# A two-block transformer on one core: the bias row spread by DRAM, three norms' roots applied after the products, padded key pairs

## The chip, the core and the metric

One core of a Trainium2 chip runs the whole program: one launch, all weights read from HBM. TensorE (PE) multiplies; VectorE (DVE), ScalarE (ACT) and GpSimd (POOL) do the elementwise work; SyncE (SP) and POOL issue most DMAs. Each engine works through its own queue in the order in which the program issues the instructions; semaphores order the queues against each other. The metric is the device time in microseconds (us), lower is better.

## What is computed

256 tokens of width 1024 in float32 go through two blocks. Cut to what matters here:

```python
# block 1
h = rms_norm(x, norm_mix_g)
u, q, keys and values (4 groups, 16 heads of 64), gates = split(h @ w_in)
conv = depthwise causal conv (31 taps), layer_norm, silu, @ conv_pw_w
s = q k / 8 + rel_bias[t5_bucket(tq - tk)]      # selected and windowed attention: 16 heads x 256 x 256
y = sigmoid(g_conv) * conv + sigmoid(g_attn) * nsa
x = x + y @ w_out
x = x + cross_attention(rms_norm(x, norm_x_g), mem)        # xq_w, xkv_w, xo_w
a, b = split(rms_norm(x, norm_ffn_g) @ ffn_in_w);  x = x + (silu(a) * b) @ ffn_out_w
x = rms_norm(x, final_norm_g)
# block 2
u, v, q, k, v2 = split(rms_norm(x, norm1_g_2) @ w_in_2)
mix = [u * spatial_gating(v), dilated_attention(rope(q), rope(k), v2)]   # 8 heads of 64
x = x + mix @ w_out_2
x = x + peer(rms_norm(x, norm2_g_2))            # 16384 experts, top 16 of 8 heads
out = rms_norm(x, final_norm_g_2)
```

A norm is `x * g / sqrt(mean(x^2) + eps)`: one factor per token, the root, and one per channel, the gain.

## The kernel before

**Products.** Float32 is split into two float32r parts, `hi` (a rounded copy) and `lo` (the rest); a product is three passes, hi*hi, hi*lo, lo*hi. The activations of a stage lie transposed (`hh`, `hl`: channels on partitions, 256 tokens in the row). `form2` makes outputs with channels on partitions (24 passes of 256 columns for a unit of weights), `form1` outputs with tokens on partitions (12 passes of 512 columns). `cols2`, `cols1` and `rows_c` run them over all units of a weight.

**The stream.** `Stream` (line 37) loads weights in chunks of 1 MB into three raw buffers; half a chunk is a unit. For each unit ACT casts `hi` (line 96) and DVE subtracts to `lo` (line 107) into one of four pairs of buffers (six from the cross-attention to w_out_2). `st.next` asks for as many units ahead as there are pairs less one, the subtraction one unit less. `st.split` does all its casts, then all its subtractions. Evacuations are put off to the next `st.next` (`st.defer`).

**The tail of a stage.** `rows_c` keeps the last four units and runs them output by output (two token blocks `tt`, two halves `hf`), then calls `finish` (line 302): `evac` adds to the residual x, multiplies by the gain into `xg` and squares with a sum; `root` gives the factor (power -0.5 on POOL, line 407) and a diagonal matrix from it (line 409); `mid` is a product in between; `turn` transposes `xg` on PE in two groups of four blocks, by multiplying with the diagonal (`by`, line 363, a float32 product in two passes) or with `ident` (line 361), then copies `hi` on ACT (line 367) and subtracts `lo` on DVE (line 368). Between the two turns stands one `st.split`, behind them another. Five stages end so: conv_pw_w (no norm), w_out (norm_x, with the product `mem_keys(3)` as `mid`), xo_w (norm_ffn), ffn_out_w (two norms one after the other, lines 1008 to 1035) and w_out_2 (norm2).

**The bias.** A product of the bias table with one-hot buckets gives a row per head (line 471). It is stored to DRAM (`b_dram`, line 477) and read back so that partition p begins at element p (`brev`, line 482). That is upside down, so eight products with a flip matrix (line 505), one per unit of w_u from the second step on, put it right. Behind the reads, in POOL's queue, stand a memset of `vpad` and the loads of the convolution's constants (`dww`, line 487, `cvec`). The convolution runs in the background on ACT (first tap, line 512) and DVE (30 taps, line 515), a few taps behind each unit.

**The scores.** `qT` and `ksw` hold two heads' channels on 128 partitions. A score product takes 64 of them, at partition 0 or 64 (lines 724 and 1148), 32 jobs in block 1 (half of them with 512 columns, half with 256) and 16 in block 2.

## Time and profile before

| | us |
|---|---|
| median of 3 runs | 1568.57 (1566.01 to 1569.83) |
| profiled execution, its own time | 1568.51 |
| its span | 1566.74 |
| PE busy | 1535.3 (98%) |
| DVE busy | 1108.8 (71%) |
| ACT busy | 830.1 (53%) |
| DMA moved | 262.79 MB, mean 168 GB/s |

A row of the trace names a line of the kernel, an engine, an operation and the tiles `out<-in`. Passes on PE overlap: from the start of one to the start of the next is less than the time from its start to its end. "Chain" rows give the time that a piece holds up the end. An arrow `<-` in brackets says what ended the idle time before an instruction. Float32 operands (not split) take two passes of PE for one product.

### The profile page before, as it was taken

How to read it: one execution, taken by the hardware profiler on the slowest of the kernel's cores; microseconds unless marked ns; L12 is line 12 of the kernel's file. 1: busy time of each engine (PE TensorE's matmuls, PEld its weight loads, DVE VectorE, ACT ScalarE, POOL GpSimd, SP SyncE). 2: the span in 40 equal slices, each digit the busy share in tenths (PEclk: the TensorE clock that was granted, in tenths of full speed). 3: DMA queues.
4: the chain of work that ended last, by engine and by line, in shares of the span. 5: the costliest groups of instructions: out<-in, count | busy, mean ns of one | idle time of the engine just before them, and what ended most of it. 6: DMA issues, size and time to landing. Idle time of an engine off the chain costs nothing.

```text
span 1566.7 us, 25104 instructions
## 1 busy us (share of the span) xinstructions
PE 1535.3 (98%) x9990; PEld 1373.9 (88%) x9990; DVE 1108.8 (71%) x2058; ACT 830.1 (53%) x1330; POOL 37.2 (2%) x75
## 2 busy tenths in 40 slices
PE   7999999999999999999999999999999999999998
PEld 7998777779799987877999999999999888888886
DVE  5887888665555555765899868999995555555555
ACT  5443565745454444465444557776664444444443
POOL 2010000000000000100000000000000000000000
PEclk9999999999999999999999999999999999999999
DMA  8454212454355563642545543433335655555552
GB/s 316 168 190 162 80 63 83 151 201 175 108 188 189 187 216 113 259 148 93 182 171 185 184 162 138 153 141 135 137 138 211 233 198 200 188 188 193 200 198 82
DMA packets 38870, 262.79 MB, mean 168 GB/s; under 512 B 4688, under 2 KB 4848, under 8 KB 8672
## 3 DMA queue, kind: packets, MB, share of 16 engines
q1 hardware_dynamic: 34992, 248.72, 44.4%
q0 software_dynamic: 2752, 9.32, 1.7%
q10 hardware_dynamic: 1008, 3.15, 0.6%
q8 instruction: 78, 1.28, 0.3%
q14 instruction: 40, 0.33, 0.1%
HBM read 257.99 MB, written 2.13 MB: 166 GB/s over the span
## 4 chain that ended last, share of the span: by engine, by line
PE 92%; DVE 4%; ACT 2%; issue 1%; DMA 1%; POOL 0%; POOLq 0%; SPq 0%; ACTq 0%; DVEq 0%
PE mm L250 41%; PE mm L270 12%; PE mm L271 12%; PE mm L272 12%; PE tp L1385 4%; PE tp L250 3%; PE tp L724 2%; PE pv L759 1%; DVE lo L107 1%; PE tp L1148 1%; PE tp L746 1%; DMA raw<-in_w_qkv_dram 0%; PE tp L1287 0%; PE tp L505 0%; ACT hi L96 0%
## 5 line engine op out<-in xcount | busy, mean ns | idle before, releaser
L96 ACT CAST hi<-raw 128x1024 fp32r<-128x1024 f32 x427 | 445.8, 1048 | 446.8 <-PE mm L272 214.4
L107 DVE TENSOR_TENSOR lo<-raw,hi 128x1024 fp32r<-128x1024 f32 x427 | 516.9, 1219 | 93.1 <-ACT hi L96 91.4
L250 PE MATMUL mm<-xnt,hi 128*128 128x256 f32 x2416 | 434.6, 282 | 9.2 <-ACT hi L96 8.6
L250 PEld LDWEIGHTS mm<-xnt,hi 128*128 128x128 f32 x2416 | 370.1, 188 | 10.3 <-ACT hi L96 8.6
L250 PE MATMUL mm<-xnt,lo 128*128 128x256 f32 x1208 | 338.0, 280 | 0.5 <-DVE lo L107 0.5
L250 PEld LDWEIGHTS mm<-xnt,lo 128*128 128x128 f32 x1208 | 227.6, 188 | 0.8 <-DVE lo L107 0.8
L270 PE MATMUL mm<-hi,wring 128*128 128x512 f32 x512 | 199.3, 389 | 1.2 <-ACT wring L243 1.2
L271 PE MATMUL mm<-lo,wring 128*128 128x512 f32 x512 | 199.3, 389 | 0.1
L272 PE MATMUL mm<-hi,wring 128*128 128x512 f32 x512 | 199.3, 389 | 0.1
L250 PE MATMUL mm<-hh,hi 128*128 128x256 f32 (+1 forms) x992 | 180.2, 283 | 1.0 <-DVE hh L368 1.0
L250 PEld LDWEIGHTS mm<-hh,hi 128*128 128x128 f32 (+1 forms) x992 | 151.5, 186 | 5.7 <-issue 4.3
L250 PE MATMUL mm<-hh,lo 128*128 128x256 f32 (+1 forms) x496 | 138.5, 279 | 0.0
L244 DVE TENSOR_TENSOR wring<-act,wring 128x512 fp32r<-128x512 f32 x64 | 44.2, 693 | 123.9 <-ACT wring L243 123.9
L270 PEld LDWEIGHTS mm<-hi,wring 128*128 128x128 f32 x512 | 96.1, 188 | 21.2 <-ACT wring L243 1.4
L271 PEld LDWEIGHTS mm<-lo,wring 128*128 128x128 f32 x512 | 96.1, 188 | 20.6 <-DVE lo L107 0.6
L272 PEld LDWEIGHTS mm<-hi,wring 128*128 128x128 f32 x512 | 96.1, 188 | 20.3 <-DVE wring L244 0.5
L515 DVE SCALAR_TENSOR_TENSOR cacc<-vpad,dww,cacc 128x256 f32<-128x256 f32 x240 | 100.9, 479 | 6.3 <-ACT cacc L512 6.3
L250 PEld LDWEIGHTS mm<-hh,lo 128*128 128x128 f32 (+1 forms) x496 | 92.6, 187 | 0.0
L1391 DVE TENSOR_TENSOR act<-act,tp 128x208 f32<-128x208 f32 (+31 forms) x64 | 57.6, 922 | 12.9 <-PE tp L1385 10.5
L270 PE MATMUL mm<-hi,hh 128*128 128x512 f32 x156 | 64.6, 414 | 0.0
L96 ACT CAST hi_x<-raw 128x1024 fp32r<-128x1024 f32 x40 | 41.9, 1051 | 41.7 <-PE mm L250 17.8
L271 PE MATMUL mm<-lo,hh 128*128 128x512 f32 x156 | 61.9, 397 | 1.5 <-DVE lo L107 1.5
(384 smaller groups left out, 2174.5 us busy)
## 6 DMA issues: line engine op xcount, KB each, us to landing
raw<-in_expert_u_dram SPq DMA_DIRECT2D x64, 1024.0 KB, 4.8
raw<-in_expert_v_dram SPq DMA_DIRECT2D x64, 1024.0 KB, 4.8
raw<-in_ffn_in_w_dram SPq DMA_DIRECT2D x22, 1024.0 KB, 4.8
raw<-in_ffn_out_w_dram SPq DMA_DIRECT2D x11, 1024.0 KB, 4.8
raw<-in_w_u_dram SPq DMA_DIRECT2D x8, 1024.0 KB, 6.6
raw<-in_w_g_dram SPq DMA_DIRECT2D x8, 1024.0 KB, 4.8
raw<-in_w_out_dram SPq DMA_DIRECT2D x8, 1024.0 KB, 4.9
raw<-in_w_query_dram SPq DMA_DIRECT2D x8, 1024.0 KB, 4.9
```

Of the source, the lines that this page charges most:

```text
L96: self.nc.scalar.copy(out=hi, in_=raw)
L107: self.nc.vector.tensor_tensor(out=lo, in0=raw, in1=hi.bitcast(F32), op=ALU.subtract)
L244: V.tensor_tensor(out=lo, in0=src, in1=hi.bitcast(F32), op=ALU.subtract)
L250: T.matmul(out=ps, lhsT=a, rhs=b, start=(k == 0), stop=(k == n - 1))
L270: T.matmul(out=ps, lhsT=a, rhs=r, start=first and k == 0, stop=False)
L271: T.matmul(out=ps, lhsT=a, rhs=q, start=False, stop=False)
L272: T.matmul(out=ps, lhsT=b, rhs=r, start=False, stop=last and k == nk - 1)
L515: V.scalar_tensor_tensor(out=cacc[:, j, :], in0=vpad[:, j, w:w + S], scalar=dww[:, j, w:w + 1], in1=cacc[:, j, :], op0=ALU.mult, op1=ALU.add)
L724: T.matmul(out=sv, lhsT=qT[po:po + 64, (g // 2) * 4 + r, tt * P:(tt + 1) * P], rhs=ksw[po:po + 64, g // 2, :, 0:n], start=True, stop=True)
L746: T.transpose(out=tps[:, o:o + P], in_=pr[:, br, c * P:(c + 1) * P], identity=ident)
L1385: T.matmul(out=ps[:, j * P:(j + 1) * P], lhsT=ring[:, b % 2, 0, j, :], rhs=ring[:, b % 2, 1, j, :], start=True, stop=True)
L1391: V.tensor_tensor(out=o[:, :, 0:there], in0=o[:, :, 0:there], in1=pv[:, :, 0:there], op=ALU.mult)
```

## The change

Three edits.

**Bias.** The table is tiled eight times, so that the product gives the row on 128 partitions (384 columns in place of 512). Eight DMAs write each head's row 128 times to DRAM, two read it back with a step of 383, which lays the bias the right way round into `bias`. The flip matrix and its eight products are gone.

**Norms.** `tail` replaces `finish` in all five stages: the first tokens are turned before the last quarter of the products. norm_x, norm_ffn and the pair behind ffn_out_w turn `x * gain` with `ident`, without the root. For the first two `row` spreads the roots along a row with a product of ones and the diagonals, and the evacuations of xq_w and ffn_in_w multiply by it; for the third the roots are per-partition scales in block 2's evacuations. With `hold` the last quarter of the turning is put off into the next stage's first product (`run_late`): half-way through the first unit of `form2`, or at the third unit of `cols1`.

**Scores.** `ksw` and `dk` keep each key twice: head 0's channels with zeros below, head 1's with zeros above; a score product contracts all 128 partitions.

```diff
+    pending = []
+
+    def run_late():
+
+        while pending:
+            pending.pop(0)()
+
...
+    def tail(pp, prod, evac, turn, root=None, after=None, mid=None, hold=False):
+
+
+
+
+
+        for hf in range(2):
+            prod(0, hf, 0, 4)
+            evac(0, hf, pp[0][hf])
+        if root is not None:
+            root(0)
+        prod(1, 0, 0, 4)
+        evac(1, 0, pp[1][0])
+        turn(0, (0, 4))
+        prod(1, 1, 0, 3)
+        st.split(max(st.n_high, st.n_used + 1))
+        if root is None:
+            turn(1, (0,))
+        prod(1, 1, 3, 4)
+        evac(1, 1, pp[1][1])
+        if root is not None:
+            root(1)
+            turn(1, (0,))
         if mid is not None:
             mid()
-        if turn is not None:
-            turn(0)
-        st.split(max(st.n_high, st.n_used + 1))
-        if turn is not None:
-            turn(1)
+        if hold:
+            pending.append(lambda: turn(1, (4,)))
+        else:
+            turn(1, (4,))
         st.split(st.n_used + st.ahead)
         st.flush()
+        if after is not None:
+            after(0)
+            after(1)
 
...
+        def after(tt):
+            rs[tt] = wk.tile([P, 1], F32, tag="rs1", name="rs1")
+            V.tensor_scalar(out=rs[tt], in0=ss[tt][:, 0:1], scalar1=ss[tt][:, 1:2], scalar2=D * EPS, op0=ALU.add, op1=ALU.add)
+            nc.gpsimd.tensor_tensor(out=rs[tt], in0=rs[tt], in1=expo[:, 0:1], op=ALU.pow)
+
+        def row(scale):
+            ps = tp_tile()
+            for tt in range(2):
+                dg = wk.tile([P, P], F32, tag="diag", name="diag")
+                V.tensor_scalar(out=dg, in0=ident, scalar1=rs[tt], scalar2=32.0 * scale, op0=ALU.mult, op1=ALU.mult)
+                T.matmul(out=ps[:, tt * P:(tt + 1) * P], lhsT=ones_1, rhs=dg, start=True, stop=True)
+            out = rrow_p.tile([P, S], F32, tag="rrow", name="rrow")
+            A.copy(out=out, in_=ps[:, 0:S])
+            return out
+
...
     b_ps = tp_tile()
-    T.matmul(out=b_ps[0:16, :], lhsT=rb, rhs=oneh, start=True, stop=True)
-    V.tensor_tensor(out=brow, in0=b_ps[0:16, :], in1=brow, op=ALU.add)
+    T.matmul(out=b_ps[:, 0:LB], lhsT=rb, rhs=oneh, start=True, stop=True)
+    V.tensor_tensor(out=brow, in0=b_ps[:, 0:LB], in1=brow, op=ALU.add)
     turn(0)
     drive(key_steps[1])
     turn(1)
-    b_dram = tc.dram_tile([16, 512], F32, name="b_dram")
-    nc.gpsimd.dma_start(out=b_dram, in_=brow)
-    b_ap = b_dram[:, :]
-    brev = []
-    for n, (pool, tag) in enumerate(((m1, "qT"), (res, "xv"))):
-        t = pool.tile([P, 8, S], F32, tag=tag, name="brev")
-        nc.gpsimd.dma_start(out=t, in_=bass.AP(tensor=b_ap.tensor, offset=b_ap.offset + n * 8 * 512, ap=[[1, P], [512, 8], [1, S]]))
-        brev.append(t)
+    b_dram = tc.dram_tile([16, P, LB], F32, name="b_dram")
+    for r in range(8):
+        nc.gpsimd.dma_start(out=b_dram[:, 16 * r:16 * r + 16, :], in_=bc(brow[16 * r:16 * r + 16, :].unsqueeze(1), [16, 16, LB]))
+    b_ap = b_dram[:, :, :]
+    for n in range(2):
+        nc.gpsimd.dma_start(out=bias[:, 8 * n:8 * n + 8, :],
+                            in_=bass.AP(tensor=b_ap.tensor, offset=b_ap.offset + n * 8 * P * LB + P - 1,
+                                        ap=[[LB - 1, P], [P * LB, 8], [1, S]]))
     vpad = m1.tile([P, KK, CW - 1 + S], F32, tag="vpad", name="vpad")
     nc.gpsimd.memset(vpad[:, :, 0:CW - 1], 0.0)
...
-            T.matmul(out=sv, lhsT=qT[po:po + 64, (g // 2) * 4 + r, tt * P:(tt + 1) * P],
-                     rhs=ksw[po:po + 64, g // 2, :, 0:n], start=True, stop=True)
+            T.matmul(out=sv, lhsT=qT[:, (g // 2) * 4 + r, tt * P:(tt + 1) * P],
+                     rhs=ksw[:, g // 2, g % 2, :, 0:n], start=True, stop=True)
...
+    ends, row = scaled_norm(x, gain_tile("norm_x_g"), nh, nl, xg)
+    rows_c("w_out", 4, yh, yl, **ends, mid=lambda: all_of(mem_keys(3, 0)))
+    rrow = row(1.0 / 16)
...
-        A.activation(out=t.rearrange("p c t -> p (c t)"), in_=ps, func=ACTF.Copy, scale=1.0 / 16)
+        V.tensor_tensor(out=t, in0=ps.rearrange("p (c t) -> p c t", c=2), in1=bc(rrow.unsqueeze(1), [P, 2, S]), op=ALU.mult)
...
+            if not rrows:
+                rrows.append(row(1.0))
+            ab = f2.tile([P, 2, S], F32, tag="ab", name="ab")
+            V.tensor_tensor(out=ab, in0=ps.rearrange("p (c t) -> p c t", c=2), in1=bc(rrows[0].unsqueeze(1), [P, 2, S]), op=ALU.mult)
             hid = f2.tile([P, S], F32, tag="hid", name="hid")
-            A.activation(out=hid, in_=ps[:, 0:S], func=ACTF.Silu)
-            V.tensor_tensor(out=hid, in0=hid, in1=ps[:, S:2 * S], op=ALU.mult)
+            A.activation(out=hid, in_=ab[:, 0], func=ACTF.Silu)
+            V.tensor_tensor(out=hid, in0=hid, in1=ab[:, 1], op=ALU.mult)
...
+    def after4(tt):
+        ssq = wk.tile([P, 2], F32, tag="ss2", name="ssq")
         r = wk.tile([P, 1], F32, tag="rs2", name="rs2")
-        V.tensor_tensor(out=t, in0=ssq[tt][:, :, 0], in1=ssq[tt][:, :, 1], op=ALU.add)
-        V.scalar_tensor_tensor(out=r, in0=t[:, 0:1], scalar=EPS, in1=t[:, 1:2], op0=ALU.mult, op1=ALU.add)
+        junk = [f1.tile([P, D], BF16, tag="junk4", bufs=2, name="junk4") for _ in range(2)]
+        A.activation(out=junk[0], in_=x[:, tt, :], func=ACTF.Square, accum_out=ssq[:, 0:1])
+        V.tensor_tensor(out=x[:, tt, :], in0=x[:, tt, :], in1=gains[0], op=ALU.mult)
+        A.activation(out=junk[1], in_=x[:, tt, :], func=ACTF.Square, accum_out=ssq[:, 1:2])
+        V.scalar_tensor_tensor(out=r, in0=ssq[:, 0:1], scalar=EPS, in1=ssq[:, 1:2], op0=ALU.mult, op1=ALU.add)
         V.tensor_scalar(out=r, in0=r, scalar1=1.0 / D, scalar2=EPS * EPS, op0=ALU.mult, op1=ALU.add)
-        nc.gpsimd.tensor_tensor(out=r, in0=r, in1=expo[:, 0:1], op=ALU.pow)
-        dgs[tt] = wk.tile([P, P], F32, tag="diag", name="diag")
-        V.tensor_scalar(out=dgs[tt], in0=ident, scalar1=r, scalar2=None, op0=ALU.mult)
-        rstd_of(t[:, 0:1], t[:, 0:1], 1.0 / D, 1)
-        r1s[tt] = t[:, 0:1]
-
-    def turn4(tt):
-        transpose_split(xg[:, tt, :], hh, hl, tt, by=dgs[tt])
-        V.tensor_scalar(out=x[:, tt, :], in0=xg1[:, tt, :], scalar1=r1s[tt], scalar2=None, op0=ALU.mult)
-
-    rows_c("ffn_out_w", DFF // 256, fh, fl_, evac=evac4, root=root4, turn=turn4)
+        nc.gpsimd.tensor_tensor(out=r2[tt][:, 0:1], in0=r, in1=expo[:, 0:1], op=ALU.pow)
+        V.tensor_scalar(out=r2[tt][:, 1:2], in0=r2[tt][:, 0:1], scalar1=0.125, scalar2=None, op0=ALU.mult)
+        rstd_of(ssq[:, 0:1], ssq[:, 0:1], 1.0 / D, 1)
+        V.tensor_scalar(out=x[:, tt, :], in0=x[:, tt, :], scalar1=ssq[:, 0:1], scalar2=None, op0=ALU.mult)
+
+    rows_c("ffn_out_w", DFF // 256, fh, fl_, evac=evac4, after=after4, hold=True,
+           turn=lambda tt, groups: transpose_split(xg[:, tt, :], hh, hl, tt, groups=groups))
...
+            if c == 2:
+                run_late()
```

## Rows read from the trace of the kernel before

**Rows 1.** Page, part 1: busy us, share of the span, instructions of each engine.
```profile
PE 1535.3 (98%) x9990; PEld 1373.9 (88%) x9990; DVE 1108.8 (71%) x2058; ACT 830.1 (53%) x1330; POOL 37.2 (2%) x75
```

**Rows 2.** Waits of PE: who waited for whom, us in total, times, longest.
```profile
PE tp L363 <- DVE rs L339: 2.4, 1, 2.4
```

**Rows 3.** Windows: length; busy of PE, PEld, DVE, ACT, POOL (instructions); granted clock, DMA, GB/s.
```profile
135.00:235.00 100.00, 99.32 (x524) 73.84 (x522) 85.25 (x245) 58.97 (x152) 0.00 (x0) 1.00 0.27 97
...
437.00:560.00 123.00, 123.00 (x1036) 122.50 (x1035) 69.15 (x87) 61.63 (x88) 0.00 (x0) 1.00 0.55 190
```

**Rows 4.** Chain that ended last, in order of time: start us, us, what.
```profile
37.13 2.83 PE mm L250 x24
...
39.95 0.86 PE tp L505 x2
...
151.38 1.05 PE tp L724 x2
...
694.66 0.63 PE tp L1148 x2
```

**Rows 5.** Timeline of PE: start us, us, engine, line, operation, out<-in, count.
```profile
376.92 1.89 PE L250 MATMUL tp<-xk,xq 128*128 128x256 f32 x8
```

**Rows 6.** Timeline of PE, then DVE, behind w_out's products (norm_x).
```profile
360.20 3.73 PE L363 MATMUL tp<-diag,xg 128*128 128x128 f32 x32
...
365.63 0.38 PE L250 MATMUL tp<-xnl,hi_x 128*128 128x256 f32 x1 [0.99 <-DVE xnl L368]
...
364.89 1.28 DVE L368 TENSOR_TENSOR xnl<-tp,xnh 128x512 fp32r<-128x512 f32 x2
...
366.08 4.62 DVE L107 TENSOR_TENSOR lo<-raw,hi 128x1024 fp32r<-128x1024 f32 x4
```

**Rows 7.** Timeline of POOL: the transfers that it issues, 24 to 30 us.
```profile
24.07 0.55 POOL L477 DMA_DIRECT2D b_dram<-brow  x1 [3.47 <-DVE brow L472]
...
27.35 1.82 POOL L482 DMA_DIRECT2D brev<-b_dram  x2 [2.73 <-DMA b_dram<-brow]
...
29.40 0.57 POOL L487 DMA_DIRECT2D dww<-in_conv_dw_w_dram  x1
```

**Rows 8.** Tiles brev, then dww: us from issue to landing.
```profile
DMA to landing us min/median/max: 7.2/9.7/12.2
...
DMA to landing us min/median/max: 12.3/12.3/12.3
```

**Rows 9.** Timeline of ACT, then DVE, at the convolution's first steps.
```profile
45.01 1.09 ACT L512 ACTIVATE cacc<-vpad,cvec,dww 128x256 f32<-128x256 f32 x2
...
45.65 1.76 DVE L515 SCALAR_TENSOR_TENSOR cacc<-vpad,dww,cacc 128x256 f32<-128x256 f32 x4 [3.14 <-ACT cacc L512]
```

**Rows 10.** DMA queues in 34 to 38 us: packets, MB, share of 16 engines.
```profile
q1 hardware_dynamic: 125, 1.02, 65.2%
...
q0 software_dynamic: 147, 0.60, 38.0%
```

**Rows 11.** Groups by line: transposes by ident; count, busy us, mean ns.
```profile
L361 PE MATMUL tp<-ident,mixo 128*128 128x128 f32 x16 | 2.4, 275 | 0.0
```

**Rows 12.** Timeline of DVE, then PE, around w_out_2's last products.
```profile
729.13 0.29 DVE L409 TENSOR_SCALAR diag<-ident,rs 128x128 f32<-128x128 f32 x1 [0.66 <-POOL rs L407]
...
730.89 1.95 PE L363 MATMUL tp<-diag,xg 128*128 128x128 f32 x16
```

**Rows 13.** Timeline of PE behind ffn_out_w's products; in brackets idle time before.
```profile
617.26 1.95 PE L363 MATMUL tp<-diag,xg 128*128 128x128 f32 x16
...
621.60 2.05 PE L363 MATMUL tp<-diag,xg 128*128 128x128 f32 x16 [2.39 <-DVE rs L339]
...
623.40 0.48 PE L270 MATMUL mm<-hi,hh 128*128 128x512 f32 x1
```

**Rows 14.** Windows: the last 4.5 us; then the chain at the start.
```profile
1562.20:1566.70 4.50, 0.00 (x0) 0.00 (x0) 0.49 (x1) 0.72 (x1) 0.01 (x1) 0.51 0.31 117
...
9.85 9.73 PE mm L250 x70
```

More of the change, by code (lines that the diff above doesn't have):

```diff
@@ L33 @@
 CF = 2048
+LB = 384
 HF = CF // 2
@@ L255, in form2 @@
         wl = w[1].rearrange("p (k n) -> p k n", k=KK)
-        pairs = []
         for k in range(KK):
-            a, b = wh[:, k, :], wl[:, k, :]
-            pairs += [(a, hh[:, k, :]), (a, hl[:, k, :]), (b, hh[:, k, :])]
-        mm3(ps, pairs)
+            if k == KK // 2:
+                run_late()
+            for n, (a, b) in enumerate(((wh, hh), (wh, hl), (wl, hh))):
+                T.matmul(out=ps, lhsT=a[:, k, :], rhs=b[:, k, :], start=k == 0 and n == 0, stop=k == KK - 1 and n == 2)
     def form1(ps, w, hh, hl, ks, nk, tt, n0, n, first, last):
@@ L330, in rows_c, with prod @@
         ws = [st.next(name, st.ahead - c) for c in range(4)]
-        for tt in range(2):
-            for hf in range(2):
-                for c in range(4):
-                    form1(pp[tt][hf], ws[c], ah, al, n - 4 + c, 1, tt, hf * 512, 512, n == 4 and c == 0, c == 3)
-        finish(pp, **ends)
+        def prod(tt, hf, c0, c1):
+            for c in range(c0, c1):
+                form1(pp[tt][hf], ws[c], ah, al, n - 4 + c, 1, tt, hf * 512, 512, n == 4 and c == 0, c == 3)
+        tail(pp, prod, **ends)
     def rstd_of(dst, ss, scale, n):
@@ L501, in tile_model @@
     nc.gpsimd.memset(cbias, NEG)
-    def bias_flip(c):
-        ps = tp_tile()
-        T.matmul(out=ps, lhsT=flip, rhs=brev[c // 4][:, 2 * (c % 4):2 * (c % 4) + 2, :].rearrange("p h k -> p (h k)"), start=True, stop=True)
-        st.defer(lambda: A.copy(out=bias[:, 2 * c:2 * c + 2, :].rearrange("p h k -> p (h k)"), in_=ps))
     cacc = m1.tile([P, KK, S], F32, tag="cacc", name="cacc")
@@ L536, in glu_evac @@
         return evac
-    flips = iter(range(8))
     for j in range(KK):
@@ L541, in tile_model @@
             run_bg(B[0])
-            c = next(flips, None) if j else None
-            if c is not None:
-                bias_flip(c)
     nc.gpsimd.tensor_copy(out=cbias[:, 0, :, 0:7], in_=bias[:, :, 159::16])
@@ L969, in tile_model, with x_prod @@
     ws = [st.next("xo_w", st.ahead - k) for k in range(2)]
-    for tt in range(2):
-        for hf in range(2):
-            for k in range(2):
-                form1(xo[tt][hf], ws[k], oh_, ol_, 6 + k, 1, tt, hf * 512, 512, False, k == 1)
+    def x_prod(tt, hf, c0, c1):
+        for k in range(c0 // 2, c1 // 2):
+            form1(xo[tt][hf], ws[k], oh_, ol_, 6 + k, 1, tt, hf * 512, 512, False, k == 1)
     hh, hl = parts_of(ht_p, "hh", False)
-    finish(xo, **residual_norm(x, gain, hh, hl, xg))
+    xg = res.tile([P, 2, D], F32, tag="xv", name="xg")
+    ends, row = scaled_norm(x, gain, hh, hl, xg)
+    tail(xo, x_prod, **ends, hold=True)
     to_dbg("x2", x)
@@ L1145, in scores @@
             tt, h = job
-            po = (h % 2) * 64
             ps = tp_tile()
-            T.matmul(out=ps[:, 0:S], lhsT=dqT[po:po + 64, 0, h // 2, tt * P:(tt + 1) * P],
-                     rhs=dqT[po:po + 64, 1, h // 2, :], start=True, stop=True)
+            T.matmul(out=ps[:, 0:S], lhsT=dq[:, h // 2, tt * P:(tt + 1) * P], rhs=dk[:, h // 2, h % 2, :], start=True, stop=True)
             if h == 0:
@@ L1213, in tile_model, with prod @@
     ws = [st.next("w_out_2", st.ahead - c) for c in range(4)]
[L1214 to L1219 removed]
     xh, xl = parts_of(xnt_p, "xnt", True)
     xg = res.tile([P, 2, D], F32, tag="xv", name="xg")
[L1222 removed]
+    def prod(tt, hf, c0, c1):
+        for c in range(c0, c1):
+            if (tt, hf, c) == (0, 1, 2):
+                transpose_split(mixo[:, 1, :], yh, yl, 1, groups=(4,))
+            form1(pp[tt][hf], ws[c], yh, yl, 4 + c, 1, tt, hf * 512, 512, False, c == 3)
+    tail(pp, prod, **residual_norm(x, gain, xh, xl, xg))
     to_dbg("x5", x)
```

135 lines of the change are left out of this document (77 added, 58 removed).

## The prediction

> **What bounds the kernel now.** I read the page first: TensorE (PE) is busy for 98% of the span [rows 1], at full granted clock. The waits of PE come next: after the start none is longer than 2.4 us [rows 2]. So a product taken away is worth its own time wherever the stage is filled with products, and a wait added is paid in full. The windows by stage say where that holds: in the attention stage VectorE (DVE) works 85.25 of 100 us beside a full PE, in the feed-forward stage 69.15 of 123 [rows 3]. Then I read the places that the change touches one by one, in order of time on each queue.
>
> **Products that go.** A flip product takes 0.86 us as a pair of passes, between units of 24 products of 2.83 us (0.118 each) [rows 4]; eight of them are 6.9 us. The product for the bias row shrinks from 512 to 384 columns: 0.2 us. A score product over 64 partitions takes 1.05 us at 512 columns, one over 128 partitions and 512 columns (the flip) 0.86 [rows 4]. At 256 columns a 64-partition pair takes 0.63 us [rows 4]; eight passes over 128 partitions in a row end after 1.89 us, so 0.216 a pass, 0.43 a pair [rows 5]. Both save 0.19 to 0.20. Of the 32 attention jobs and 16 dilated jobs, 48 x 0.194 = 9.3 us. PE fills those stages, so I take all of it; with 6.2 us less in the attention stage DVE rises to about 90%, and if that costs a third of its part, 2 us are lost. Sum: -16.4, between -13 and -16.5. The padding zeros (POOL memsets) and the two half copies for one on ScalarE (ACT) hide under PE. So does one 512-wide DVE pass for each of 22 feed-forward steps, some 0.69 us each [rows 6], 15 us in a stage where DVE has 54 free [rows 3]; without that cover it would cost those 15.
>
> Here a rule of the skill speaks against the change. The Trainium skill, "TensorE: Matmul & The Clock Gate" (Why this matters for your kernels), has a single matmul over 32 rows take as long as one over 128. By it the padding saves nothing. This trace disagrees, 0.63 against 0.43 us.
>
> **The bias detour by DRAM.** Today POOL sends a 32 KB row to DRAM at 24.07, reads 2 MB back at 27.35, and then issues the convolution's weights `dww` at 29.40 [rows 7]; these land 12.3 us later, at 41.7 [rows 8], behind the reads on the same queue. After the change eight writes of 384 KB (3.15 MB) come first, and both reads wait for all of them; `dww` is queued behind. Who waits: the first convolution step on ACT (line 512), which ran at 45.01, and behind it on ACT each cast `hi`, behind its taps on DVE each `lo` [rows 9]. Without three flips ACT gets there at 45.0 - 3 x 0.86 = 42.4. The stream casts three units ahead and subtracts two ahead, so at that moment PE is in its sixth unit of w_u and has that one and two more: its fourth unit starts at 37.13 less one flip, 36.27 [rows 4], so the ninth, whose `lo` is missing, at 36.27 + 5 x 2.83 = 50.4.
> When `dww` lands: the 2 MB of reads took until 28.3 + 12.2 = 40.5 [rows 7, 8], 13 us, some 2.5 of them before data moved, so 0.2 MB/us beside the weight stream; 3.15 MB by that need 16 + 2.5 us, to 42.5. Then from first read to landed `dww` 14.3 us as now, or 4 less if the weight stream has dried up: 53 to 57. I take 55. PE goes on after the convolution step and its semaphore (0.65), four taps (1.76) [rows 9] and one `lo` (1.22): 55 + 3.65 - 50.4 = 8.3 us of stall. DVE then has 1.14 + 1.67 + 0.2 = 3.0 us of work for units of 2.83, and no lead left: 1.5 more by the end of the stage. Sum +9.8. If all moved at the best rate that a window shows, both queues' 1.62 MB in 4 us [rows 10], `dww` would land near 44: no stall. With writes at half the software queue's share of now (38% [rows 10]) it is 62: +16.5.
> On that share: in this window the software queue moved 147 packets and the weight queue 125 [rows 10], for 0.60 against 1.02 MB. The Trainium skill, "DMA: Bandwidth & Descriptors" (Queues, rings and completion order), says each engine takes turns between queues packet by packet. The trace agrees, and rows of 1.5 KB would then get the lower share; by the rule the sum is that of the bound, 1588.
>
> **The five tails.** `finish` evacuated everything, then turned; `tail` turns the first tokens before the last quarter of the products. Where the chain after the last product sets the end, that hides nothing. I walk each in queue order; a 512-wide pass costs 0.64 to 0.69, a 1024-wide one 1.14, each in a row of them [rows 6]; a turned block of 128x128 takes one pass where `ident` is used (16 blocks, 16 passes [rows 11]) and two passes of 0.112 with the diagonal (32 in 3.73 us [rows 6]).
> - conv_pw_w and xo_w: turning the first tokens moves ahead of the last quarter, but DVE then still has their two `lo` and a split before the last evacuation, and PE waits for that either way; +0.2 and +0.65 (0.45 of it the four passes of the new row product); bound -1 to +2 together.
> - w_out (norm_x): now 32 passes from 360.20, first full-rate product at 365.63 [rows 6]; the filler before it waits 1 us for a `lo` and would end at 359.1 without, so 6.4 are spent. New: eight of the blocks lie before, four are turned before the last quarter, the filler ends at 360.4, the last four blocks at 360.8. Then `row` stands in PE's queue ahead of the queries, and it needs the diagonals, which need `after`, which stands in DVE's queue behind the held half's `lo` and five splits: 362.5 + 5 x 1.14 = 368.3; two sums (0.2 each), two roots on POOL (0.66 each with the hops [rows 12]), a diagonal (0.29): 370.1. Queries start at 370.4, against 365.5: +4.9, and PE idles 9.5 us.
> - ffn_out_w: now from 617.26 to 623.40 [rows 13], 6.1 us. New: last product at 618.6, and w_uv runs at once for the first tokens and half of the second: two units and a half, with four turned blocks, to 626.0. The held half is turned at its third unit, but its copy and `lo` stand behind three splits, all of `after4` and the casts of three more units. On DVE: the turned quarter's `lo` to 619.3, the last evacuation to 620.6, three `lo` to 624.0, then the product with the gain to 625.2. Meanwhile ACT casts three units to 621.5 and squares the first block to 622.7; its second square waits for that product, 626.4; sums, the two roots one after the other and the scaling take DVE and POOL to 629.1. The second token block goes the same way (its first square is out early) and ends at 634.1. ACT, free at 631.4, casts three units and copies the held half to 635.0; DVE does two `lo`, 636.4, and the held one, 637.0. By then the old order has done 59 products of this stage, the new one 33: 26 x 0.231 = +6.0, with 9 us idle.
> - w_out_2 (norm2, diagonal kept): the diagonal of the first tokens ends at 729.42 [rows 12], but PE would now use it before the last quarter, 12 x 0.227 ahead of 730.89 [rows 12], at 728.17: 1.4 idle with the hop, then 1.8 of turning, both before the last quarter. The chain behind the last product stays as long as it is: +3.2.
> Sum +14.9, between +8 and +18.
>
> **The clock.** In the last 4.5 us, in which PE does nothing, the mean granted clock is 0.51 [rows 14], its lower level, 1.2 of 2.4 GHz. At the start 70 products take 9.73 us [rows 14] for 8.26 at 0.118: 1.5 us lost before full speed. Today's stages between show 1.00 [rows 3], with no wait above 2.4 us in them. I price each of the three stalls of 8 to 9 us at those 1.5: +4.5, between 0 (the level holds) and +7.
>
> **How the numbers follow.** The profiled execution took 1568.51 us (span 1566.74 and 1.8 around it), the median of the runs 1568.57. -16.4 + 9.8 + 14.9 + 4.5 = +12.8: 1581 us.
> Rivals:
> - `dww` lands in time. For it: idle stretches of the weight stream; against: 5.2 MB ahead of it on one queue. Decides at a landing of 46.7. -16.4 + 14.9 + 3.0 = +1.5: 1570. Chance 0.2 (same 0.65, slower 0.25, faster 0.1).
> - Faster: the two tails at 360 and 618 don't stall because their waits are out before DVE's splits. Place: `row` in norm_x and the held half in w_uv; if the last diagonal is there by 361.5 and the held `lo` by 627, these tails give 3.5 and 4.4 instead of costing 10.9, and the clock holds there: 12.8 - 18.8 - 3.0 = -9: 1559.5. For it: DVE is only half busy there; against: the queue's order. It decides as soon as PE's idle there falls below some 4 us in each. Chance 0.13 (0.8 of it faster).
> - The padding does nothing (64 rows weren't what made those products long): +9.3 on the forecast, 1590.5. Against: two widths show the same 0.19. Chance 0.06.
> - The forecast's own case, 1574 to 1592: 0.55. The rest, 0.06, I spread.
> By over 0.3%, about what a measurement of this kernel can tell from no change (1563.9 and 1573.3): faster 0.14, same 0.19, slower 0.67. Range, with the bounds of detour, tails and clock: 1564 to 1593.
>
> **What would show it.** Right: 128-partition scores at 0.86 and 0.43 a pair; `dww` landed after 50 and PE waiting for `lo` near 50; PE idle 9 us ahead of the row product near 350 and in the third unit of w_uv; a clock below full after each. Wrong: line 512 near 42.4 without a wait, or `after` ahead of the splits on DVE.

## The result, and the profile after

The changed kernel takes 1582.8 us (median of 6 runs, 1576.3 to 1584.4) where the kernel before takes 1567.3 beside it: ratio 1.0087, 95% interval 1.0068 to 1.0106. By that ratio it is 13.6 us slower (the two medians lie 15.5 apart); forecast were 12.8. The profiled execution has a span of 1581.2 us against 1566.7, 14.5 more.

Part 1 of the page of the changed kernel answers to [rows 1]: fewer instructions on PE, less busy time, a smaller share of a longer span. What was taken from PE came back as idle time.

```profile
PE 1516.2 (96%) x9934; PEld 1374.4 (87%) x9934; DVE 1125.6 (71%) x2081; ACT 826.5 (52%) x1316; POOL 45.0 (3%) x86
```

The waits of PE (who waited for whom, us in total, times, longest), where [rows 2] showed 2.4 as the longest after the start:

```profile
PE mm L268 <- DVE lo L108: 15.1, 3, 14.4
PE mm L278 <- ACT xnt L395: 8.8, 1, 8.8
PE tp L479 <- DVE diag L478: 8.6, 1, 8.6
...
PE tp L391 <- DVE diag L437: 2.9, 1, 2.9
```

The first is the `lo` behind the convolution, the second the held quarter in w_uv, the third the row product of norm_x, the fourth w_out_2. Three of the four stand where the prediction put them.

To see what each stage did, I took the start of every weight product in both traces and subtracted: how late the changed kernel is at the same product (its "offset" below). The differences between the ends of the stages:

| stage | forecast, with its clock | measured |
|---|---|---|
| to the end of w_u (103 us) | -7.1 + 9.8 + 1.5 = +4.2 | +8.7 |
| attention (to 262) | -6.2 | -10.0 |
| conv_pw_w and gates | +0.2 | +1.3 |
| w_out, norm_x | 4.9 + 1.5 = +6.4 | +6.2 |
| xo_w | +0.65 | +1.8 |
| ffn_out_w and w_uv | 6.0 + 1.5 = +7.5 | +8.6 |
| block 2's attention | -3.1 | -4.9 |
| w_out_2 | +3.2 | +2.8 |
| sum | +12.8 | +14.5 |

So the total was right with two larger errors of opposite sign in it: w_u, with the detour, came out 4.5 dearer than forecast, and the two attention stages with the padded keys 5.6 cheaper.

Timelines of the changed kernel at the detour (POOL, then ACT, DVE and PE; in brackets the idle time before and what ended it), to lay beside [rows 7 to 9]:

```profile
23.80 4.51 POOL L539 DMA_DIRECT2D b_dram<-brow  x8 [3.35 <-DVE brow L533]
51.35 1.78 POOL L542 DMA_DIRECT2D bias<-b_dram  x2 [23.04 <-DMA b_dram<-brow]
...
53.36 0.56 POOL L548 DMA_DIRECT2D dww<-in_conv_dw_w_dram  x1
...
61.21 1.09 ACT L568 ACTIVATE cacc<-vpad,cvec,dww 128x256 f32<-128x256 f32 x2 [14.70 <-DMA cvec<-in_conv_dw_b_dram]
...
63.89 1.21 DVE L108 TENSOR_TENSOR lo<-raw,hi 128x1024 fp32r<-128x1024 f32 x1
...
65.15 0.58 PE L268 MATMUL mm<-hh,lo 128*128 128x256 f32 x1 [14.36 <-DVE lo L108]
```

POOL waits 23.0 us for the writes, `dww` lands 7.5 us after its issue, at 60.9, and then the chain is the one forecast: first convolution step, four taps, one `lo`, PE. (What ended ACT's wait by the profile is the load of `cvec`, which POOL issues right behind `dww`.) PE's last pass began at 50.5, and PE ran dry at 50.8 (65.15 less 14.36).

The granted clock, by windows (length; busy of PE, PEld, DVE, ACT, POOL with instructions; granted clock, DMA, GB/s): 0.50 is the lower of the two levels, 1.2 GHz.

```profile
66.00:68.00 2.00, 2.00 (x11) 2.00 (x11) 2.00 (x4) 0.00 (x0) 0.30 (x2) 0.50 0.03 8
...
330.00:332.00 2.00, 2.00 (x7) 1.61 (x6) 0.80 (x2) 1.67 (x3) 0.98 (x2) 0.50 0.29 23
...
370.00:372.00 2.00, 2.00 (x11) 2.00 (x10) 0.11 (x1) 1.32 (x2) 0.00 (x0) 0.50 0.68 279
...
442.00:444.00 2.00, 2.00 (x12) 2.00 (x11) 0.97 (x1) 0.99 (x1) 0.00 (x0) 0.50 0.65 160
...
646.00:648.00 2.00, 2.00 (x6) 1.52 (x6) 0.27 (x1) 0.69 (x1) 1.91 (x3) 0.50 0.96 339
...
750.00:752.00 2.00, 2.00 (x11) 1.99 (x11) 0.97 (x2) 1.56 (x3) 0.00 (x0) 0.50 0.48 197
```

These are six places, the detour and all five new tails; the prediction had counted three. In the chain of the changed kernel, passes of 512 columns behind conv_pw_w's tail take 0.43 in place of 0.23, and 35 passes of 256 behind xo_w's take 5.87 in place of 4.13 at 0.118:

```profile
330.29 0.43 PE mm L278
...
440.49 5.87 PE mm L268 x35
```

### The profile page after: what moved, and what is told of

The parts are those of the page before. It is cut to its first block, busy times and chain, and to the rows that moved or that the text cites. A ratio compares the mean times of both kernels' runs of the same rounds, so it can differ in the third digit from the quotient of the medians.

```text
span 1581.2 us, 25016 instructions
## 1 busy us (share of the span) xinstructions
PE 1516.2 (96%) x9934; PEld 1374.4 (87%) x9934; DVE 1125.6 (71%) x2081; ACT 826.5 (52%) x1316; POOL 45.0 (3%) x86
## 3 DMA queue, kind: packets, MB, share of 16 engines
q10 hardware_dynamic: 1008, 3.15, 0.7%
## 4 chain that ended last, share of the span: by engine, by line
PE 86%; DVE 6%; DMA 3%; ACT 2%; issue 1%; POOL 1%; SPq 0%; POOLq 0%; ACTq 0%; DVEq 0%
PE mm L268 36%; PE mm L280 12%; PE mm L279 12%; PE mm L278 12%; PE tp L1478 4%; DVE lo L108 2%; DVE cacc L571 2%; PE tp L258 2%; PE tp L268 2%; DMA b_dram<-brow 1%; PE tp L789 1%; PE pv L824 1%; DMA gain<-in_norm_mix_g_dram 1%; PE tp L811 1%; PE tp L389 0%
## 5 line engine op out<-in xcount | busy, mean ns | idle before, releaser
L268 PE MATMUL mm<-hh,hi 128*128 128x256 f32 x976 | 173.1, 281 | 4.2 <-DVE hh L396 2.4
L268 PEld LDWEIGHTS mm<-hh,hi 128*128 128x128 f32 x976 | 150.3, 191 | 5.9 <-DVE hh L396 3.0
L268 PE MATMUL mm<-hh,lo 128*128 128x256 f32 x488 | 137.2, 281 | 14.7 <-DVE lo L108 14.7
L268 PEld LDWEIGHTS mm<-hh,lo 128*128 128x128 f32 x488 | 92.7, 190 | 15.1 <-DVE lo L108 15.1
L1478 PE MATMUL tp<-raw 128*128 128x128 f32 x512 | 62.3, 275 | 0.0
L1478 PEld LDWEIGHTS tp<-raw 128*128 128x128 f32 x512 | 59.8, 192 | 0.0
```

Of the source, the lines that this page charges most:

```text
L268: T.matmul(out=ps, lhsT=a[:, k, :], rhs=b[:, k, :], start=k == 0 and n == 0, stop=k == KK - 1 and n == 2)
L1478: T.matmul(out=ps[:, j * P:(j + 1) * P], lhsT=ring[:, b % 2, 0, j, :], rhs=ring[:, b % 2, 1, j, :], start=True, stop=True)
```

## Experiments

The edits are shown in short; `...` and remarks behind `#` stand for code that is left out.

### The detour: where the constants stand in POOL's queue

Theory: the landing of `dww` behind the writes makes the stall. Rival: the transfers themselves do, wherever `dww` stands.

```diff
+    vpad, dww, cvec, cm0, bd16, cpos, cw2, ones_c, cbias   # tiles, memsets and loads, unchanged
     b_dram = tc.dram_tile([16, P, LB], F32, name="b_dram")
     for r in range(8): ...
     for n in range(2): ...
-    vpad, dww, cvec, cm0, bd16, cpos, cw2, ones_c, cbias
```

> The changed kernel with the convolution's constants (dww, cvec and the six small loads and memsets behind them) issued on POOL ahead of the eight writes of the bias instead of behind its two reads. Theory, order on POOL's queue: dww lands before 42 us, the first convolution step runs near 42.4 without a wait, PE's 14.4 us stall at 50.5 and the 1.3 us at half clock behind it go: 15.7 less than the changed kernel, some 1567 us, no difference from the kernel before (ratio 0.998 to 1.002). Rival, the transfers themselves: 5.2 MB of writes and reads still share the DMA engines with the weight stream, the casts of w_u wait for raw chunks instead (they already waited 4.2 and 2.0 us in the changed kernel), and a stall of 5 us or more stays near 50 to 60: 1573 us or more. Third, DVE: with no lead lost but 30 taps a step at work, PE gets behind by 1 to 2 us over the stage: 1568.5.

Measured: ratio 0.9987 (0.9975 to 0.9999), 1566.1 us. The whole stall is gone, 15.7 us (1.0087 less 0.9987 of 1567). Timelines of POOL and ACT:

```profile
21.18 0.59 POOL L540 DMA_DIRECT2D dww<-in_conv_dw_w_dram  x1
...
46.49 1.05 ACT L97 CAST hi<-raw 128x1024 fp32r<-128x1024 f32 x1 [5.63 <-DMA raw<-in_w_u_dram]
47.45 1.09 ACT L567 ACTIVATE cacc<-vpad,cvec,dww 128x256 f32<-128x256 f32 x2
```

`dww` lands 2.9 us after its issue. The rival isn't nothing: the writes do make a chunk of w_u late, ACT waits 5.6 us for it, and the first step runs at 47.45, not at the expected 42.4. But PE still has units ahead, and that wait ends before they do. The order in the queue was the cause.

The bias edit alone, with that order, prices the flips:

```diff
 # the kernel before, with the bias edit of the change and the constants first
-            bias_flip(c)
```

> The kernel before with the bias edit alone, and the convolution's constants issued ahead of the bias's writes. Theory: the eight flip products (6.9) and the shorter row product (0.2) go, and with dww out of the writes' way nothing of the detour reaches PE: 6 to 7 less than the kernel before, 1561.5 us, ratio 0.9958. Rival, the 5.2 MB beside the weight stream and the earlier start of DVE's taps take it back within the stage: ratio 0.999 to 1.000.

Measured: ratio 0.9972 (0.9960 to 0.9984), 4.4 us; between the two. By the offsets of the trace it is 6.2 ahead at 57 us, near the flips' price, but 5.3 at 75. The same in the kernel with the constants first; its windows show DVE without a gap from 60 to 100, where the kernel before had 7.81 of 10 at the end (its row first):

```profile
90.00:100.00 10.00, 10.00 (x87) 10.00 (x87) 7.81 (x16) 5.11 (x7) 2.27 (x4) 1.00 0.51 196
...
90.00:100.00 10.00, 9.78 (x83) 9.57 (x82) 10.00 (x19) 3.78 (x5) 2.68 (x6) 1.00 0.73 251
```

There PE waits for DVE: 1.5 us of the flips' 6.9 goes back by 100 us (4.7 ahead). That is the third case of the expectation for the constants first, a small one. In this one trace another 1.6 goes at 168 us, where the granted clock falls to 0.50 without a wait (see the end); it ends 2.5 ahead, and the timing over 12 runs has 4.4.

### What makes the writes slow

I had taken 16 us plus 2.5 for the 3.15 MB, from the rate of today's reads. From the first issue at 23.80 to POOL's release at 51.35 they took 27.5 (23.0 of it is POOL's wait behind the last issue).

```diff
-        nc.gpsimd.dma_start(out=b_dram[:, 16 * r:16 * r + 16, :], ...)
+        nc.scalar.dma_start(out=b_dram[:, 16 * r:16 * r + 16, :], ...)
```

> The changed kernel with the eight writes of the bias issued by ACT (hardware queue) in place of POOL (software queue); reads, dww and all else stay on POOL, behind the writes as before. In the changed kernel the writes took 23.0 us, and moved 105 to 175 GB/s even at 26 to 32 us, while the weight queue was idle. Theory A, the software queue is the limit: writes done near 38 us in place of 51, dww lands near 48, the stall of 14.4 at 50.5 shrinks to 3 or less: 10 less than the changed kernel, 1572 us, ratio 1.003. Theory B, the transfer itself is (128 copies a row, read from 16 partitions a DMA): writes still take 20 us or more from issue, dww lands within 3 us of 60.9, 0 to 3 gained; up to 4 lost if the eight issues on ACT hold back casts: 1580 to 1587 us.

Measured: ratio 1.0103 (1.0088 to 1.0118), 1586.3 us. Theory B for the writes: they take 21.3 us from the first issue, 28.36, to POOL's release at 49.68. Its second part missed: `dww` landed at 66.4, not within 3 us of 60.9. DMA queues (packets, MB, share of 16 engines): first the changed kernel at 26 to 30 us, then the changed kernel at 34 to 38, where the weight stream runs beside, then this one at 38 to 42, then this one's issues on ACT.

```profile
q0 software_dynamic: 162, 0.61, 98.5%
q1 hardware_dynamic: 20, 0.04, 2.6%
```

```profile
q1 hardware_dynamic: 128, 0.97, 57.1%
q0 software_dynamic: 177, 0.62, 43.9%
```

```profile
q10 hardware_dynamic: 526, 0.76, 93.9%
```

```profile
28.36 15.01 ACTq L539 DMA_DIRECT2D b_dram<-brow  x8
```

These rows of 1536 bytes move at 150 to 190 GB/s (0.61 and 0.76 MB in 4 us), on either queue. No other queue was in the way at 26 to 30 us, and with the weight stream beside them at 34 to 38 the writes moved as much, 0.62 MB. So it was not a share between queues that I got wrong, but the price of the transfer itself. Nor does the share of the engines' time tell that price: it is 98.5% alone and 43.9% beside the weights, for the same 0.6 MB. The Trainium skill, "DMA: Bandwidth & Descriptors" (Queues, rings and completion order), with its turns packet by packet, doesn't explain a rate that low in a window with one busy queue. The size of a packet alone doesn't set it either: 3.8 KB on the mean on POOL's queue, 1.4 KB on ACT's, which was the faster. Whether it is the row length or that each transfer reads 16 partitions only, no run here separates. ACT's queue spent 15.0 us on the eight issues (POOL: 4.51), and casts stood behind them, as the expectation had allowed: PE waited 7.1 us for `hi` at 44.5, and 8.8 for `lo` later.

### The padded keys alone

```diff
-            T.matmul(out=sv, lhsT=qT[po:po + 64, ...], rhs=ksw[po:po + 64, g // 2, :, 0:n], ...)
+            T.matmul(out=sv, lhsT=qT[:, ...], rhs=ksw[:, g // 2, g % 2, :, 0:n], ...)
```

> The kernel before with the padded keys alone (both attentions), and the smaller buffers that make room for them (two pT for three, no cpT, narrower junk). Theory, a score product over 128 partitions takes 0.43 and 0.86 us where one over 64 takes 0.63 and 1.05: 48 x 0.194 = 9.3 less than the kernel before, 1558 us, ratio 0.9940; 7.3 (0.9953) if DVE, closer to its limit, gives a third of the attention part back. Rival, the page's rule that the rows in use don't set the time of a product: ratio 1.000, pairs still 0.63 and 1.05. Second rival, the two pT for three make PE wait for a copy: less than 5 gained, with new waits of PE on ACT's pT.

To make room, this kernel also has two buffers of `pT` for three and no `cpT`; PE shows no wait for `pT`, so the second rival is out.

Measured: ratio 0.9939 (0.9925 to 0.9953), 9.6 us, what the forecast had. The parts have other sizes, though. Chain at the score products (start us, us, what), first one of 512 columns and one of 256 in the kernel before, then the same two with padded keys:

```profile
152.43 3.02 PE mm L250 x24
...
201.24 0.63 PE tp L724 x2
201.86 0.43 PE mm L270
```

```profile
151.61 2.83 PE mm L250 x24
...
197.61 0.49 PE tp L736 x2
198.10 0.23 PE mm L270
```

The pair goes from 0.63 to 0.49, not to 0.43: the row of eight passes that I priced it by ([rows 5]) has no other product between them. But the pass behind the product over 64 partitions shows 0.43 where it shows 0.23 now. That is 0.34 a job in this part. Where 24 passes of 256 columns follow, as at 151 us, the product gives the 0.19 forecast (1.05 to 0.86), and the passes behind it another 0.19. The ends of matmuls are modelled, so only the sum over product and successors is sure, not how they share it. By the offsets of the traces the attention stage gives 9.5 (forecast 6.2), 0.3 for each of its 32 jobs, and block 2's part 3.6 (3.1). The timing sees 9.6 of these 13.1, with an interval of about 2 to either side; the profiled execution was the fastest of the six. DVE took nothing back that shows. The Trainium skill, "TensorE: Matmul & The Clock Gate" (Why this matters for your kernels), would have had no gain here; both the ratio and these rows decide against that for products over 64 partitions of this form.

### norm_x: the roots ahead of DVE's splits

The rival that would have made the change faster had its place here: diagonals out before the `lo` of the splits.

```diff
         evac(1, 1, pp[1][1])
+        after(0); after(1); diag(0); diag(1)     # w_out alone
         if mid is not None:
             mid()
```

> The changed kernel with norm_x's two sums, roots and diagonals issued right behind the last evacuation of w_out, ahead of the product for the memory keys and of DVE's splits; everything else as in the changed kernel. Theory, queue order on DVE: DVE is idle there from 356.9 to 361.3, so the diagonals are out near 359, before PE gets to the row product at 360.4; the 8.6 us wait and the half pace behind it (1.3) go: 9 to 10 less than the changed kernel, 1573 us, ratio to the kernel before 1.0035, and this tail becomes some 3.5 faster than the one before. Rival, only the place of the wait changes: DVE's waits for the squares and for POOL's roots hold back the splits behind them, and PE waits for lo in the second or third query instead: 3 or less gained, 1580 us.

Measured: ratio 1.0045 (1.0029 to 1.0061), 1575.0 us: 6.6 less than the changed kernel, of 9 to 10 expected. Timelines of DVE and PE:

```profile
358.30 0.29 DVE L479 TENSOR_SCALAR diag<-ident,rs 128x128 f32<-128x128 f32 x1 [0.22 <-POOL rs L475]
...
360.59 0.61 PE L486 MATMUL tp<-diag,ones 128*128 128x128 f32 x4
362.37 0.39 PE L268 MATMUL tp<-xnh,hi_x 128*128 128x256 f32 x1 [1.17 <-ACT hi_x L97]
363.63 0.39 PE L268 MATMUL tp<-xnh,lo_x 128*128 128x256 f32 x1 [0.76 <-DVE lo_x L108]
```

The second diagonal is out at 358.6 and the row product waits for nothing, so the order in DVE's queue was the cause of the 8.6. The first query's second pass, at 365.63 in the kernel before ([rows 6]), starts 3.0 us earlier, near the 3.5 that the rival was priced with. But 2.4 of that are gone five microseconds later (offset -3.0 at 362.6, -0.6 at 367.7): 0.8 in a wait for `lo_x`, and 1.6 behind it, where the windows have the granted clock at 0.57 and 0.58 and the kernel before holds 1.00.

```profile
364.00:366.00 2.00, 2.00 (x13) 2.00 (x12) 2.00 (x3) 2.00 (x3) 0.00 (x0) 0.57 0.30 45
366.00:368.00 2.00, 2.00 (x13) 2.00 (x12) 2.00 (x2) 1.81 (x4) 0.00 (x0) 0.58 0.81 311
```

So at norm_x the rival's condition is met (the last diagonal out by 361.5) and its gain is there at first, but the clock doesn't hold, which it had assumed.

### The clock by itself

```diff
+    scrap = tp_tile()
+    for n in range(9):
+        T.matmul(out=scrap, lhsT=ident, rhs=xg[:, 0, 0:512], start=True, stop=True)
     rrow = row(1.0 / 16)
```

> The changed kernel with nine extra products of 512 columns (float32, 0.86 us each, 7.7 us in all, their result is not used) in PE's queue ahead of norm_x's row product, where PE waits 8.6 us for the diagonals. They measure the clock by itself: same diagonals, same time of the row product, but PE busy until then. Theory, the half pace behind that wait comes from PE's idleness: granted clock 1.00 at 368 to 374 us instead of 0.50 to 0.60, the first query's passes 0.118 apart, and 1.3 to 1.5 less from there on. Rival, the queries are slow for another reason (lo, weight loads): same pace, no gain. If the extra products hold back the diagonals' engines nothing should change, since these are DVE and POOL.

Measured in the trace: chain at the row product, in the changed kernel, then with the wait filled.

```profile
369.29 1.21 PE tp L479 x4
370.50 5.57 PE tp L268 x35
```

```profile
367.01 0.90 PE tp L479 x4
367.91 6.13 PE tp L268 x52
```

A pass takes 0.159 on the mean in the first and 0.118 in the second, and the row product 0.31 less: 35 x 0.041 + 0.31 = 1.7 us. By the offsets it is 1.5. The granted clock of the window 370 to 372 is 1.00 with the wait filled. Here PE's idleness lowered the clock, and 1.5 us a stall was a fair price for one place. (The span of this single run, 1572.7, is 8.5 shorter: 2.5 lay ahead of this place already, and 4.3 came from another pace of the feed-forward stage, see the end.)

### ffn_out_w: three steps to what really held PE

First the hold alone, taken away:

```diff
-    rows_c("ffn_out_w", ..., after=after4, hold=True, turn=...)
+    rows_c("ffn_out_w", ..., after=after4, turn=...)
```

> The changed kernel without the hold in ffn_out_w's tail alone: the last quarter is turned in the tail, before the splits and the four squares and roots of the two norms, which stay where they are. Theory, the held copy stood behind that work in ACT's and DVE's queues: the 8.8 us wait in the third unit of w_uv goes, a wait of about 2 us for the last evacuation comes in the tail, and at the sixth unit PE may wait 0 to 2.5 us for a lo that stands behind the same chain: 5 to 8 less than the changed kernel, 1576 us, ratio to the kernel before 1.0055. Rival, the chain of the two norms itself (10 us on DVE with waits for ACT and POOL) blocks the lo of whatever comes next, held or not: a wait of 6 us or more shows two or three units later, and 2 or less is gained: 1581 us.

Measured: ratio 1.0087 (1.0068 to 1.0107), no gain. The rival. Timelines of PE and DVE:

```profile
629.32 0.63 PE L389 MATMUL tp<-ident,xg 128*128 128x128 f32 x4 [2.12 <-DVE xg L1101]
...
646.34 0.50 PE L279 MATMUL mm<-lo,xnt 128*128 128x512 f32 x1 [2.43 <-DVE lo L108]
...
662.62 0.80 PE L279 MATMUL mm<-lo,xnt 128*128 128x512 f32 x1 [5.06 <-DVE lo L108]
...
654.84 0.69 DVE L1157 TENSOR_TENSOR vn<-vn,gv 128x512 f32<-128x512 f32 x1 [2.74 <-DMA gv<-in_ln_v_g_dram]
```

The two small waits are the expected ones, and at 640 us this kernel is 10.5 ahead of the changed one. Then a wait that I had not listed takes nearly all of it back: DVE stands for the constants `gv` of the gating norm, whose loads POOL issues behind the roots of `after4`, and with DVE the `lo` stand. In the changed kernel that was hidden behind the stall.

Second, without the hold, the norms' work taken apart and put where DVE and ACT are idle:

```diff
+    squares4(0) behind evac(0, 1); roots4(0) behind evac(1, 0)
+    squares4(1) behind the last turned quarter; roots4(1), scales4 behind the splits
```

> The changed kernel without the hold in ffn_out_w's tail, and with the two norms' work taken apart and spread: the first tokens' squares and gain product behind their own evacuation, their roots behind the third evacuation, the second tokens' squares behind the last turned quarter, only their roots and the scalings behind the splits. Theory, what cost 8.6 there was the serial chain of squares and roots (10 us) ahead of lo in DVE's queue, and behind it the constants of block 2 in POOL's queue (a wait of 5.1 us in the run without the hold): DVE reaches the lo of w_uv's sixth unit 6 us earlier than in that run and POOL the loads of gv as well; PE keeps one wait of 2 us for the last evacuation: 9 to 10 less than the changed kernel, 1573 us, ratio to the kernel before 1.0035. Rival, the loads of gv stay late (their space is free only when the squares are done) and the wait of 3 to 5 us for them stays: 1577 to 1578 us, ratio 1.0065. Second rival, DVE's early waits for ACT and POOL delay the turning of the first tokens: new waits of PE in the tail, 1579 or more.

Measured: ratio 1.0044 (1.0023 to 1.0065), 6.7 less than the changed kernel: between theory and rival. PE's wait for the `lo` behind `gv` is 3.5 us here. Third, on top of that, the order of POOL's loads:

```diff
+    gv512 = s1.tile(...); 4 loads
     rope, dmask, wsT, bsT: 4 loads
-    gv512 = s1.tile(...); 4 loads
```

> The spread norms in ffn_out_w's tail, and in POOL's queue the four loads of gv ahead of the four loads of rope, dmask, wsT and bsT. Theory: what was left there, a wait of 3.5 us for lo and some 2 before it at half pace, came from DVE's wait for gv (1.4 and 2.7 us); 2.6 us of issues fewer stand before it: 2 to 3 less than the run with the spread norms, 1574 us, ratio 1.0028. Rival, the raw chunks of w_qkv are late by then (ACT waited 2.3 to 6.3 us for them) and the wait for lo stays: ratio 1.0044.

Measured: ratio 1.0011 (0.9996 to 1.0025), 5 less again, more than expected. DVE no longer waits at that line:

```profile
642.56 0.69 DVE L1179 TENSOR_TENSOR vn<-vn,gv 128x512 f32<-128x512 f32 x1
```

By the offsets the wait gives 4 to 5; so the late raw chunks of w_qkv were a consequence of it, not a limit of their own. All three covers together (the held copy, the serial chain of squares and roots, the loads behind it in POOL's queue) were needed to explain this tail; the prediction named the first two.

### w_out_2 in the old order

```diff
+        if root is not None:      # all products and evacuations, then
+            turn(0); st.split(...); turn(1); ...
```

> The changed kernel with the old order in the tail of w_out_2 alone: all products, then both token blocks turned with their diagonals. Theory: the first diagonal is out before the last quarter ends, so PE's 2.9 us wait for the second diagonal falls to some 1.1, with the 16 blocks of the first tokens' turning in front of it, and the granted clock of 0.50 seen at 750 to 752 us stays 1.00: 2.6 less than the changed kernel, span 1578.5. Rival, the wait is the chain of the last tokens and doesn't depend on what is turned when: span within 0.5 of 1581.

Measured in the trace: the offset to the changed kernel moves by 2.8 us at this tail (-4.6 ahead of it, -7.3 behind; the 4.6 are the other pace of the feed-forward stage again). The wait for the second diagonal in PE's waits, and the window at its place:

```profile
PE tp L403 <- DVE diag L449: 1.1, 1, 1.1
```

```profile
744.00:748.00 4.00, 4.00 (x34) 4.00 (x35) 3.75 (x4) 3.62 (x4) 1.08 (x2) 1.00 0.26 65
```

More than half of the gain is the clock, which holds: in the changed kernel the 16 blocks of the second turning take 2.60 where those of the first take 2.02, and the nine passes behind them 2.16 in place of 1.06 at 0.118, 1.7 us together.

```profile
747.80 2.60 PE L391 MATMUL tp<-diag,xg 128*128 128x128 f32 x16 [2.88 <-DVE diag L437]
```

### Versions that beat both

All repairs in one kernel, and then only what the runs spoke for:

```diff
 # best: constants first, norm_x's roots early, norms of ffn_out_w spread, no hold in xo_w, old order in w_out_2
 # best2: constants first, padded keys, norm_x's roots early; the other four tails and their norms as before
```

> The changed kernel with the five repairs together: constants ahead of the bias's writes, norm_x's roots ahead of the memory product, ffn_out_w's norms spread and not held, the old order in w_out_2's tail, and xo_w's last quarter not held. Theory, the repairs are in different stages and add up: 1582.8 - 15.7 - 8 - 9.7 - 2.6 - 0.5 = 1546 us, ratio to the kernel before 0.9865 (padding 9.4, flips 6 of it). Rival, what one stage gains the next gives back since the weight stream is at its limit there (raw chunks late): 1552 us or more, with waits of ACT's hi for raw.

> What the runs speak for and nothing else: the padded keys, the bias spread by DRAM with the constants ahead of it, norm_x's root behind the products with its diagonals issued early; the tails of conv_pw_w, xo_w, ffn_out_w and w_out_2 and their norms as in the kernel before. Theory, sum of the parts: 9.4 (padding) + 6.2 (flips) + 2 (norm_x): 17.6 less than the kernel before, 1550.5 us, ratio 0.9888. Rival, the parts compete for the DMA engines and for DVE in the first stages, as far as the five repairs together gave 0.9907 in place of 0.9865: 1556 us or more.

Measured: the first 0.9907 (0.9888 to 0.9927), 1553.6 us; the second 0.9881 (0.9866 to 0.9895), 1551.0. The first misses its sum by 6 to 7: its tails in xo_w and ffn_out_w keep new waits of 3.6 and 2.6 us (PE for `xg`) and 3.4 for `lo` (it still has `gv` last in the queue), and its granted clock is 0.50 from 414 to 418 and from 636 to 640. The second meets its sum, since four of its tails are the old ones, at full clock. Its page:

```profile
PE 1516.5 (98%) x9962; PEld 1373.9 (89%) x9962; DVE 1109.9 (72%) x2062; ACT 825.1 (53%) x1323; POOL 44.4 (3%) x86
```

PE is as busy as in the changed kernel (1516) and again 98% of the span. Between it and the kernel with only the constants first lie 1.06%, 16.6 us: the price of the four new tails with their norms and of norm_x's late roots, which are 6 to 7 of it.

## Why the prediction was right, point by point

- *What bounds the kernel.* Right: new waiting was paid (the detour's 14.4 of PE idle went with 15.7 of time), and products taken away were gained as long as DVE kept up.
- *Flip products, 6.9.* Right in the trace (6.2 ahead at 57 us); 4.4 by timing. DVE has no gap in the second half of w_u once PE is earlier, and 1.5 goes back there. The 2 us that I allowed DVE I had put into the attention stage; what shows of them belongs to w_u.
- *Score products, 0.194 each.* Mechanism right, size of the term wrong twice: the pair in its surroundings 0.49 and mostly 0.91 in place of 0.43 and 0.86, and 0.2 more from what follows it, which I hadn't looked at; together 0.3 a job. The row was there to read: in the kernel before, the pass at 201.86 takes 0.43.
- *Bias detour, 8.3 of stall.* The place (PE dry at 50.8, forecast 50.4), the queue and the steps behind the landing (4.25 us, forecast 3.65) were right. The failed step is "0.2 MB/us": reads that ran beside the weight stream priced writes of another form, which moved 0.15 (0.61 MB in 4 us). Writes done at 51.35 in place of 42.5; then reads and `dww` came in 9.5 us where I took 12.5; `dww` at 60.9 in place of 55, and the stall 14.4. The bound of 62 held it by luck: it was worked out for a halved share of the DMA engines, and the writes moved as much beside the weights as alone.
- *DVE's lag of 1.5 behind the detour.* Not seen behind the stall: the changed kernel is 9.8 late at 77 us and 8.7 at 103.
- *norm_x.* Right to a microsecond: diagonal at 369.65 (forecast 370.1), PE idle 8.6 (9.5), cause confirmed by the roots put early.
- *ffn_out_w.* The walk through the queues gave the held `lo` at 637.0; it ended at 645.1 in a kernel that came 8.0 late to this tail, so at 637.1. Right in mechanism and size, but incomplete: the loads of `gv` behind the same chain stood hidden under the stall.
- *The clock, 1.5 a stall.* The price was right, 1.5 to 1.7 by the filled wait. The failed step is the count: "each of the three stalls of 8 to 9 us", with waits up to 2.4 us taken as harmless because they are in the kernel before. It fell in six places.
- *conv_pw_w and xo_w.* +3.1 where +0.85 was forecast. The clock is more than the difference: six passes at 0.43 in place of 0.23 in the first (1.2 us), 35 at 0.168 in place of 0.118 in the second (1.7).
- *w_out_2, 3.2.* Measured 2.8, but 1.7 of it is clock, so the waiting alone was forecast too high by 2.
- *Rivals.* `dww` in time: no. The faster case: met in norm_x by another order, but the clock took its gain back. No effect of the padding: no.

The sum came close because errors cancel, and that is luck: by the table, w_u came out 4.5 dearer and conv_pw_w, xo_w and ffn_out_w 1.1 each, the two attention stages 5.6 cheaper and w_out_2 0.4. A forecast by single terms, with rows for each, was needed to see that afterwards.

## What to carry to other kernels

A DMA that is put ahead in a queue delays every small load behind it: ask first which of those a step near the critical path reads, and issue that one earlier. When a wait is taken away, look for what it hid; here three covers lay over one another at one tail, each a queue (ACT, DVE, POOL) in which something needed soon stood behind something needed later. Price a product with the instruction behind it, not alone.
